# Filter taps from split operands, and the embedding's product moved from the state space scan to its set-up

## The chip, the cores and the metric

The kernel runs on one core of a Trainium2 chip. The metric is the device time of one launch in microseconds (us). The kernel before took 3740.24 us, the median of three runs (3736.25 to 3745.21). All other times here come from one further execution that the hardware profiler recorded.

## The reference, cut to what matters

One encoder layer over 2048 tokens of width 1024. After a norm, one input projection feeds four token mixers; their outputs go through an output projection, a feed-forward block and a gated per-layer embedding. Three pieces touch the change.

```python
def hyena_filter_spectrum(l, w1, b1, w2, b2, w3, log_decay):
    ...
    hid = jnp.sin(feats @ w1.astype(f32) + b1.astype(f32))
    hid = jnp.sin(hid @ w2.astype(f32) + b2.astype(f32))
    h = hid @ w3.astype(f32)                       # the filter taps: [2048, 64] @ [64, 1024]
    h = h * jnp.exp(-jnp.exp(log_decay.astype(f32))[None, :] * t[:, None])
    ...

# s5_mixer: the state space layer (set-up of the discretised matrices, then the scan)
# reference:
        gate = jax.nn.sigmoid(rmsnorm(h, g_ple[i]) @ w_ple_gate[i])
        h = h + gate * (p[i] @ w_ple[i])           # the embedding's product: [2048, 256] @ [256, 1024]
```

`p @ w_ple` depends on inputs alone, so it can be computed at any time before the last stage.

## The kernel before, in words

The program runs in three stretches. First the input projection (class `InProj`), then attention (class `Attention`) for the differential and the latent heads together, then output projection, feed-forward block and gated embedding, which all go through seven-product (Strassen) block multiplications. Attention works in 64 blocks, one head and 128 query rows each: 20 score products, 32 transposes and 32 weighings (each weighing shows as two pieces in the trace). With head h the keys and values are loaded again, so a head changes after every 16 blocks.

A float32 operand is often split into two parts, `hi` (rounded to the format float32r) and `lo` (the rest). A product of two split operands is then three products of parts (`mm3`, L52 to L54), each one piece on TensorE. A product of two unsplit float32 operands is issued once and shows as two pieces in the trace.

Beside the projection and the attention runs a queue of six background jobs (class `Background`). Each is a Python generator that yields estimated costs. At each of its steps, the main job lets the first job in the queue advance by a credit (`RATES`: 5.0 and 8.0 during the projection, 1.2, 1.2, 1.0 and 2.0 during attention). The jobs are the Hyena filters, the latent attention's preparation, the state space set-up with the short convolution, the state space main part (the scan, its output products and its gate) with the embedding, the Hyena long convolution, and the splitting of the output weights. `together(main, make, ..., every)` joins a second job to a first: after every `every`-th yield of the first, the second yields once, and what is left of the second runs when the first is done.

The framework then schedules all instructions by priority in a simulated timeline and fixes the order on each engine. TensorE (PE), VectorE (DVE), ScalarE (ACT), GpSimd (POOL) and SyncE (SP, which issues most DMAs) each execute in that order, so an instruction that waits holds up all that stand behind it on its engine.

Names used below: `f_hid` is the filters' hidden layer and `f_w` its weights (taps: L1113). `s5m_rows` holds the state space inputs loaded from DRAM (L1510), `s5m_u` their rearranged copy (ACT, L1522), transposed on PE at L1528. `d_s_m<-d_s_g` (L1507) are 16 DRAM-to-DRAM copies that spread the set-up's result. Scan instructions are L1567 to L1585 on POOL. The embedding's product is L52 to L54 on `wp_hi`/`wp_lo` and `pT_hi`/`pT_lo`, with transposes of `p_rows` (L946), copies into the tile `emb` (ACT, L954) and stores to DRAM (`d_emb`, L955). `emb` has one buffer.

Of the kernel before, what the change touches and what calls it, by code (L numbers as in the profile page):

```python
# [19 lines left out]
SEQ = 2048  # L20
# [1041 lines left out]
def hyena_filters(ops, const, A, S, cp, wk, ps_pool):  # L1062

    tc, nc = ops.tc, ops.nc
    dft = Dft16(ops, wk, 128, [nc.vector if e else nc.gpsimd for e in ENG[0]])
    feats = wk.tile([33, SEQ], F32, name="feats", tag="hy_a")
    nc.sync.dma_start(feats, A["c_feats"])
    w1 = cp.tile([33, 64], F32, name="f_w1")  # L1070
    nc.sync.dma_start(w1, A["hy_f_w1"][0])
    w2 = cp.tile([64, 64], F32, name="f_w2")
    nc.sync.dma_start(w2, A["hy_f_w2"][0])
    w3 = cp.tile([64, 1024], F32, name="f_w3")
    nc.sync.dma_start(w3, A["hy_f_w3"][0])
    bb = cp.tile([64, 2], F32, name="f_b")
    nc.sync.dma_start(bb[:, 0:1], A["hy_f_b1"][0].rearrange("(p o) -> p o", o=1))
    nc.sync.dma_start(bb[:, 1:2], A["hy_f_b2"][0].rearrange("(p o) -> p o", o=1))
    times = cp.tile([128, 16], F32, name="f_times")
    nc.sync.dma_start(times, A["c_times"])  # L1080
    ones = cp.tile([128, 128], F32, name="f_ones")
    nc.vector.memset(ones, 1.0)
    hid = cp.tile([64, SEQ], F32, name="f_hid")
    for layer, (w, src) in enumerate(((w1, feats), (w2, hid))):
        z = wk.tile([64, SEQ], F32, name="f_z", tag="hy_b")
        for c in range(4):
            ps = ps_pool.tile([128, 512], F32, name="ps_hy", tag="ps_hy")[:64]
            nc.tensor.matmul(ps, lhsT=w, rhs=src[:, ts(c, 512)], start=True, stop=True)
            nc.vector.tensor_scalar(z[:, ts(c, 512)], ps, bb[:, layer : layer + 1], None, ALU.add)
        for c in range(2):  # L1090
            k = wk.tile([64, 1024], F32, name="f_k", tag="f_mat", bufs=2)
            reduce_angle(nc, z[:, ts(c, 1024)], k)
        nc.scalar.activation(hid, z, AF.Sin)
        yield 10.0
    w3v = w3.rearrange("p (o d c) -> p o d c", o=2, d=2)

    def taps(od, hh):

        eld = wk.tile([128, 2, 128], F32, name="f_eld", bufs=1)
        for d in range(2):  # L1100
            nc.sync.dma_start(eld[:, d], A["hy_log_decay"][0:1, ds(512 * od + 256 * d + 128 * hh, 128)]
                              .to_broadcast([128, 128]))
        nc.scalar.activation(eld, eld, AF.Exp)
        h = wk.tile([128, 16, 2, 128], F32, name="f_h", tag="hy_a")
        part = wk.tile([128, 256], F32, name="f_part", bufs=1)
        nc.gpsimd.memset(part, 0.0)
        done.append((h, part))
        for t2 in range(8):
            ps = ps_pool.tile([128, 512], F32, name="ps_hy", tag="ps_hy")
            e = wk.tile([128, 512], F32, name="f_e", bufs=2)  # L1110
            for tt in range(2):
                t = 2 * t2 + tt
                nc.tensor.matmul(ps[:, ts(tt, 256)], lhsT=hid[:, ts(t, 128)], rhs=w3v[:, od, :, ts(hh, 128)],  # L1113
                                 start=tt == 0, stop=True, skip_group_check=True)
                nc.scalar.activation(e[:, ts(tt, 256)], eld.rearrange("p d c -> p (d c)"), AF.Exp,
                                     scale=times[:, t : t + 1])
            part_h = h[:, ts(t2, 2)].rearrange("p t d c -> p (t d c)")
            nc.vector.tensor_mul(part_h, ps, e)
            if t2 == 0:
                nc.vector.memset(h[0:1, 0, 1], 0.0)  # L1120
            nc.scalar.activation(e, part_h, AF.Abs)
            for tt in range(2):
                nc.gpsimd.tensor_add(part, part, e[:, ts(tt, 256)])
            yield 1.2

    done, groups = [], [(od, hh) for od in range(2) for hh in range(2)]
    yield from taps(*groups[0])
    for n, (od, hh) in enumerate(groups):
        h, part = done.pop()
        ps = ps_pool.tile([128, 512], F32, name="ps_hy", tag="ps_hy")[:, 0:128]  # L1130
        for d in range(2):
            nc.tensor.matmul(ps, lhsT=ones, rhs=part[:, ts(d, 128)], start=d == 0, stop=d == 1)
        skip = wk.tile([1, 128], F32, name="f_skip", bufs=1)
        nc.sync.dma_start(skip, A["hy_skip"][0, od : od + 1, ts(hh, 128)])
        norm = wk.tile([128, 128], F32, name="f_norm", bufs=1)
        nc.vector.tensor_copy(norm, ps)
        inv = wk.tile([128, 128], F32, name="f_inv", bufs=1)
        nc.vector.reciprocal(inv, norm)
        nc.vector.tensor_mul(norm[0:1], norm[0:1], skip)
        nc.vector.tensor_add(h[0:1, 0, 0], h[0:1, 0, 0], norm[0:1])  # L1140
        yield 6.0
        z = wk.tile([128, 2, 16, 128], F32, name="f_spec", tag="hy_b")
        for b in range(4):
            for a in range(2):
                f = wk.tile([128, 2, 4, 128], F32, name="f_mat", tag="f_mat", bufs=2)
                nc.sync.dma_start(f, A["c_dft_f"][:, b + 4 * a :: 8])
                ps = ps_pool.tile([128, 512], F32, name="ps_hy", tag="ps_hy").rearrange(
                    "p (t r c) -> p t r c", t=2, r=2)
                for i in range(2):
                    t = b + 4 * a + 8 * i  # L1150
                    for r in range(2):
                        mm = nc.tensor.matmul
                        mm(ps[:, i, r], lhsT=f[:, i, r], rhs=h[:, t, 0], start=i + r == 0, stop=False,
                           skip_group_check=True)
                        mm(ps[:, i, r], lhsT=f[:, i, 2 + r], rhs=h[:, -t % 16, 1], start=False,
                           stop=True, skip_group_check=True)
                for i in range(2):
                    nc.vector.tensor_mul(z[:, :, b + 4 * a + 8 * i], ps[:, i],
                                         inv[:, None, :].to_broadcast([128, 2, 128]))
                yield 2.0  # L1160
            eng = dft.engines[b]
            s = wk.tile([128, 2, 4, 128], F32, name="f_s", bufs=1)
            yield from dft.four(eng, z[:, :, b::4], s, False)
            if b:
                dft.rotate(eng, z[:, :, b::4], s, b, False)
                yield 2.0

        ahead = taps(*groups[n + 1]) if n < 3 else iter(())
        for ka in range(4):
            s = wk.tile([128, 2, 4, 128], F32, name="f_s", bufs=1)  # L1170
            for cost in dft.four(dft.engines[ka], z[:, :, ts(ka, 4)], s, False):
                yield cost
                yield next(ahead, 0.0)
            for r in range(2):
                nc.sync.dma_start(S["hspec"][od, hh, r, ka::4].rearrange("b p c -> p b c"), z[:, r, ts(ka, 4)])
        yield from ahead
# [537 lines left out]
def tile_hybrid_encoder(ctx, tc, A, out):  # L1714
# [19 lines left out]
    def background(make, c_name, w_name, side=None):  # L1734
        def gen():
            with ExitStack() as c:
                small = pool(c, c_name, 1, side=side)
                work = pool(c, w_name, 1, side=side)
                yield from make(ops, const, A, S, small, work, bg_ps)
        return gen  # L1740

    ip, st = InProj(ops, A, S), Strassen(ops)
    with ExitStack() as ac:
# [6 lines left out]
        def together(main, make, c_name, w_name, every):  # L1750

            def gen():
                with ExitStack() as c:
                    side = make(ops, const, A, S, pool(c, c_name, 1, side="right"), pool(c, w_name, 1, side="right"), bg_ps)
                    for n, cost in enumerate(main()):
                        yield cost
                        if n % every == 0:
                            yield next(side, 0.0)
                    yield from side
            return gen  # L1760
# [1 line left out]
        bg = Background(tc)  # L1762
        bg.add(background(hyena_filters, "hf_c", "hf_w", "right"))
        bg.add(background(mla_prep, "mp_c", "mp_w", "right"))
        bg.add(together(background(s5_setup, "ss_c", "ss_w", "right"), hyena_conv, "hc_c", "hc_w", EMN[1]))
        bg.add(together(background(s5_main, "sm_c", "sm_w", "right"), embedding, "em_c", "em_w", EMN[0]))
        bg.add(background(hyena_main, "hm_c", "hm_w", "right"))
        bg.add(out_weights)
        ip.run(const, bg.advance, lambda: bg.until(4))
# [119 lines left out]
```

## Time and profile before

| | |
|---|---|
| median of three runs | 3740.24 us |
| profiled execution, own time | 3744.99 us |
| its span, first to last instruction | 3743.2 us |
| TensorE busy | 3423.1 us (91%) |
| VectorE busy | 2455.0 us (66%) |
| ScalarE busy | 1754.3 us (47%) |
| GpSimd busy | 1553.0 us (41%) |
| mean granted TensorE clock | 0.958 of full |

Busy time is the sum of recorded spans; matmuls overlap in the array, so what one costs the stream is the distance from its start to the next one's start and not its own duration. The input projection takes the time up to about 555 us, attention runs from there to about 1900 us, and the rest follows. In the order of time the background jobs are the filters (to 391 us), the latent preparation (to 584 us), set-up and short convolution (585 to 850 us), scan and embedding (850 to 1216 us), long convolution (1216 to 1620 us) and output weights (1620 to 1700 us).

### The profile page before, as it was taken

Reading aid. Unit: us, or ns where it says so; the run is one execution under the profiler, and the core shown is the slowest. Engines: PE = TensorE matmul, PEld = TensorE weight load, DVE = VectorE, ACT = ScalarE, POOL = GpSimd, SP = SyncE. Lnnn points to the kernel's source line nnn. Section 1 sums busy time; section 2 is a strip of 40 time slices with the busy share of each in tenths; the row PEclk is TensorE's granted clock in tenths of the full one; section 3 lists DMA queues with packets and bytes.
Section 4 is the critical chain, followed back from the end, with each engine's and each line's share of the span. In section 5 each row is a group of like instructions: output and inputs, shape, how many; then the busy total and the mean of one; then the engine's idle time right before and its main releaser. Section 6 shows DMA issues by size and latency. Waiting matters only on the chain. (4 is left out here: it accounts for less than half of the span.)

```text
span 3743.2 us, 56824 instructions
## 1 busy us (share of the span) xinstructions
PE 3423.1 (91%) x20582; PEld 2802.2 (75%) x20582; DVE 2455.0 (66%) x5109; ACT 1754.3 (47%) x2889; POOL 1553.0 (41%) x1423
## 2 busy tenths in 40 slices
PE   8999997887999899989999899999999987989787
PEld 6889875676778778767777678887888865867666
DVE  6667548974746455677667764447545578688877
ACT  5334316665667545577754443334333433333443
POOL 1324001681852022253355554445544544344554
PEclk9999997998999999999999899999999999999899
DMA  4544655327232795961054532223222254546554
GB/s 143 185 142 153 219 164 141 104 76 208 76 100 87 190 251 146 222 195 40 18 178 144 177 113 79 90 79 107 90 79 90 74 188 149 203 141 191 186 170 151
DMA packets 426698, 518.46 MB, mean 139 GB/s; under 512 B 117003, under 2 KB 319631, under 8 KB 422415
## 3 DMA queue, kind: packets, MB, share of 16 engines
q1 hardware_dynamic: 352368, 407.05, 36.8%
q10 hardware_dynamic: 74048, 107.76, 8.2%
q8 instruction: 163, 2.67, 0.3%
q14 instruction: 119, 0.97, 0.1%
HBM read 340.89 MB, written 178.01 MB: 139 GB/s over the span
## 5 line engine op out<-in xcount | busy, mean ns | idle before, releaser
L448 PE MATMUL ps_s<-k_sb,q_sb 96*128 96x512 f32 x1280 | 437.5, 444 | 53.8 <-DVE at_s L451 22.2
L823 PE MATMUL ps_st<-t_hi,s_hi 128*128 128x512 f32 x984 | 397.2, 404 | 51.8 <-DVE st_sum L850 21.2
L458 ACT ACTIVATE at_s<-at_s,least_s 128x2048 f32<-128x2048 f32 x192 | 384.2, 2003 | 88.3 <-DVE least_s L457 71.6
L453 DVE CUSTOM_DVE_ANT_0 at_s<-ps_s,strip 128x512 f32<-128x512 f32 x512 | 338.1, 685 | 111.2 <-PE ps_s L448 96.9
L823 PE MATMUL ps_st<-t_lo,s_hi 128*128 128x512 f32 x984 | 392.6, 399 | 10.3 <-DVE t_lo L41 10.2
L823 PE MATMUL ps_st<-t_hi,s_lo 128*128 128x512 f32 x984 | 391.7, 398 | 5.6 <-DVE s_lo L41 5.5
L40 ACT ACTIVATE s_hi<-s_raw 128x512 fp32r<-128x512 f32 (+1 forms) x336 | 206.8, 618 | 352.9 <-PE ps_st L823 290.4
L497 ACT ACTIVATE at<-ps_at 128x512 f32<-128x512 f32 x512 | 287.7, 595 | 164.0 <-PE ps_at L492 151.1
L472 POOL TENSOR_SCALAR at_s<-at_s,f 128x1024 f32<-128x1024 f32 (+1 forms) x48 | 89.9, 1872 | 659.9 <-DVE f L466 474.6
L41 DVE TENSOR_TENSOR s_lo<-s_raw,s_hi 128x512 fp32r<-128x512 f32 (+1 forms) x336 | 270.0, 806 | 137.7 <-ACT s_hi L40 137.5
L492 PE MATMUL ps_at<-ident,at_s 128*128 128x128 f32 x2048 | 318.4, 286 | 41.7 <-ACT at L497 31.8
L40 ACT ACTIVATE a_hi<-a_raw 128x512 fp32r<-128x512 f32 (+1 forms) x252 | 155.4, 618 | 403.2 <-PE ps_st L823 217.5
L492 PEld LDWEIGHTS ps_at<-ident,at_s 128*128 128x128 f32 x2048 | 250.9, 146 | 108.5 <-ACT at L497 43.4
L448 PEld LDWEIGHTS ps_s<-k_sb,q_sb 96*128 96x128 f32 x1280 | 230.6, 197 | 122.4 <-DVE at_s L451 37.4
L823 PE MATMUL ps_st<-b_hi,a_hi 128*128 128x512 f32 x656 | 263.8, 402 | 30.9 <-DVE st_row L912 12.3
L807 POOL TENSOR_TENSOR s_raw<-a_raw 128x512 f32<-128x512 f32 (+1 forms) x84 | 110.8, 1319 | 433.6 <-DMA a_raw<-d_g 148.7
L41 DVE TENSOR_TENSOR a_lo<-a_raw,a_hi 128x512 fp32r<-128x512 f32 (+1 forms) x252 | 235.3, 936 | 72.1 <-ACT a_hi L40 71.1
L502 PE MATMUL ps_o<-at,v_sb 128*64 128x128 f32 x4096 | 274.2, 287 | 4.4 <-ACT at L497 3.3
L823 PEld LDWEIGHTS ps_st<-t_hi,s_hi 128*128 128x128 f32 x984 | 190.4, 194 | 104.4 <-DVE st_sum L850 25.0
L502 PEld LDWEIGHTS ps_o<-at,v_sb 128*64 128x64 f32 x4096 | 239.5, 144 | 36.2 <-issue 23.3
L823 PE MATMUL ps_st<-b_lo,a_hi 128*128 128x512 f32 x656 | 261.3, 398 | 4.4 <-DVE b_lo L41 4.3
L823 PE MATMUL ps_st<-b_hi,a_lo 128*128 128x512 f32 x656 | 260.7, 397 | 0.0
(480 smaller groups left out, 8305.7 us busy)
## 6 DMA issues: line engine op xcount, KB each, us to landing
d_h<-st_row ACTq DMA_DIRECT2D x64, 512.0 KB, 3.2
st_row<-d_h SPq DMA_DIRECT2D x64, 512.0 KB, 4.3
a_raw<-in_w_gate_dram SPq DMA_DIRECT2D x44, 512.0 KB, 4.0
a_raw<-in_w_up_dram SPq DMA_DIRECT2D x44, 512.0 KB, 3.9
d_g<-st_row ACTq DMA_DIRECT2D x44, 512.0 KB, 2.9
f_mat<-in_c_dft_f_dram SPq DMA_DIRECT2D x32, 512.0 KB, 4.4
h_g<-in_c_hy_g_dram SPq DMA_DIRECT2D x32, 512.0 KB, 7.1
h_sp<-d_hspec SPq DMA_DIRECT2D x64, 256.0 KB, 6.9
```

The lines of the kernel that those rows point to most:

```text
L40: nc.scalar.activation(hi, src, AF.Copy)
L41: nc.vector.tensor_sub(lo, src, hi.bitcast(F32))
L448: nc.tensor.matmul(ps, lhsT=lhs, rhs=rhs[:, ts(c, 512)], start=n == 0, stop=n == len(products) - 1)
L453: nc.vector.tensor_tensor_reduce(dst, ps, at.strip[:, ds(1920 - 128 * self.t + 512 * c, 512)], self.slope, 3e38, ALU.add, ALU.min, least)
L458: nc.scalar.activation(s, s, AF.Exp, bias=least, scale=-1.0, accum_out=self.total[name])
L472: nc.gpsimd.tensor_scalar(s2[:, n:], s2[:, n:], f, 0.0, ALU.mult, ALU.add)
L492: self.turned[hd, g] = nc.tensor.transpose(ps[:, j], src[:, ts(4 * g + j, 128)], at.ident)
L497: nc.scalar.activation(tile, ps, AF.Copy)
L502: mm = lambda out, lhsT, rhs, first, last: nc.tensor.matmul(out, lhsT=lhsT, rhs=rhs, start=first, stop=last, skip_group_check=True)
L807: eng.tensor_add(s1, a21, a22)
L823: nc.tensor.matmul(bank, lhsT=l[x][:, c], rhs=r[y], start=first and c + k == 0, stop=c == kb - 1 and k == 2, skip_group_check=True)
```

## The change

Two edits that do not depend on each other.

First, the taps. The second hidden layer's weight is loaded twice side by side, so that this product gives the 64 hidden values twice, on partitions 0 to 63 and 64 to 127. After the sine a copy rounds all 128 rows to float32r; on the upper 64 rows the rounded value is then subtracted, which leaves the low part there. The last weight is no longer loaded whole: each of the four groups of taps loads its 256 columns twice, rounds them (`w_hi`, 128 rows) and forms the low part (`w_lo`, 64 rows). One product over 128 rows gives (hi + lo) times `w_hi`, one over 64 rows adds hi times `w_lo`.

Second, the queue. The embedding is joined to set-up and short convolution, no longer to the state space main part, which now runs alone.

```diff
-    w2 = cp.tile([64, 64], F32, name="f_w2")
-    nc.sync.dma_start(w2, A["hy_f_w2"][0])
-    w3 = cp.tile([64, 1024], F32, name="f_w3")
-    nc.sync.dma_start(w3, A["hy_f_w3"][0])
...
+    w2 = cp.tile([64, 128], F32, name="f_w2")
+    bb = cp.tile([128, 2], F32, name="f_b")
+    nc.sync.dma_start(bb[0:64, 0:1], A["hy_f_b1"][0].rearrange("(p o) -> p o", o=1))
+    for half in range(2):
+        nc.sync.dma_start(w2[:, ts(half, 64)], A["hy_f_w2"][0])
+        nc.sync.dma_start(bb[ts(half, 64), 1:2], A["hy_f_b2"][0].rearrange("(p o) -> p o", o=1))
...
-        nc.scalar.activation(hid, z, AF.Sin)
+        nc.scalar.activation(z, z, AF.Sin)
         yield 10.0
-    w3v = w3.rearrange("p (o d c) -> p o d c", o=2, d=2)
+    hid = cp.tile([128, SEQ], F32R, name="f_hid")
+    nc.scalar.activation(hid, z, AF.Copy)
+    low = hid[64:128]
+    nc.vector.tensor_tensor(low, z[64:128], low.bitcast(F32), ALU.subtract)
...
+        w = wk.tile([128, 256], F32, name="f_w3", bufs=1)
+        for half in range(2):
+            nc.sync.dma_start(w[ts(half, 64)].rearrange("k (d c) -> k d c", d=2),
+                              A["hy_f_w3"][0].rearrange("k (o d c) -> k o d c", o=2, d=2)[:, od, :, ts(hh, 128)])
+        w_hi, w_lo = wk.tile([128, 256], F32R, name="f_w3_hi", bufs=1), wk.tile([64, 256], F32R, name="f_w3_lo", bufs=1)
+        nc.scalar.activation(w_hi, w, AF.Copy)
+        nc.vector.tensor_tensor(w_lo, w[0:64], w_hi.bitcast(F32)[0:64], ALU.subtract)
...
-                nc.tensor.matmul(ps[:, ts(tt, 256)], lhsT=hid[:, ts(t, 128)], rhs=w3v[:, od, :, ts(hh, 128)],
-                                 start=tt == 0, stop=True, skip_group_check=True)
+                nc.tensor.matmul(ps[:, ts(tt, 256)], lhsT=hid[:, ts(t, 128)], rhs=w_hi,
+                                 start=tt == 0, stop=False, skip_group_check=True)
+                nc.tensor.matmul(ps[:, ts(tt, 256)], lhsT=hid[0:64, ts(t, 128)], rhs=w_lo,
+                                 start=False, stop=True, skip_group_check=True)
...
-        bg.add(together(background(s5_setup, "ss_c", "ss_w", "right"), hyena_conv, "hc_c", "hc_w", EMN[1]))
-        bg.add(together(background(s5_main, "sm_c", "sm_w", "right"), embedding, "em_c", "em_w", EMN[0]))
+        short = together(background(s5_setup, "ss_c", "ss_w", "right"), hyena_conv, "hc_c", "hc_w", EMN[1])
+        bg.add(together(short, embedding, "em_c", "em_w", EMN[0]))
+        bg.add(background(s5_main, "sm_c", "sm_w", "right"))
```

How this moves the instructions shows in the fixed order. On PE, in the first half of the projection, where the first taps stand (`ps_ip` are the projection's own products, `ps_tr` the transposes of its input), before:

```order
L54 MATMUL ps_ip<-w_hi,aT_lo 128x304
L1113 MATMUL ps_hy<-f_w_368,f_hid 128x256 x4
L98 MATMUL ps_tr<-ident,x_in 128x128 x8
L1113 MATMUL ps_hy<-f_w_368,f_hid 128x256 x4
L52 MATMUL ps_ip<-w_hi,aT_hi 128x304
```

and in the changed kernel:

```order
L52 MATMUL ps_ip<-w_hi,aT_hi 128x304
L1124 MATMUL ps_hy<-f_w_hi,f_hid 128x256 x2
L1126 MATMUL ps_hy<-f_w_lo,f_hid 128x256
L1124 MATMUL ps_hy<-f_w_hi,f_hid 128x256
L1126 MATMUL ps_hy<-f_w_lo,f_hid 128x256 x2
L1124 MATMUL ps_hy<-f_w_hi,f_hid 128x256
L1126 MATMUL ps_hy<-f_w_lo,f_hid 128x256
L98 MATMUL ps_tr<-ident,x_in 128x128 x4
```

The order counts a float32 product once (the trace shows two pieces of it), so 64 products of taps become 128 and 128 pieces stay 128.

On SP, where the state space main part begins, before (`k_sb` and `v_sb` are the next head's keys and values, `s5m_win` and `s5m_m` the scan's matrices, `d_s_g<-s_strip` the set-up's last stores):

```order
L1496 DMA d_s_g<-s_strip 16x496
L1516 DMA s5m_bglu<-in_s_b_glu_dram 128x256
L369 DMA k_sb<-d_kda 32x2048 x2
L1507 DMA d_s_m<-d_s_g 16x16x256 x16
L1510 DMA s5m_rows<-d_zs_58 128x4096
L1535 DMA s5m_win<-d_s_win 128x1024 x2
L369 DMA k_sb<-d_kda 32x2048
L371 DMA k_sb<-d_kmn 64x2048
L392 DMA v_sb<-d_vda 128x8x64
```

and in the changed kernel:

```order
L381 DMA q_sb<-d_qda 32x2x128 x3
L382 DMA q_sb<-d_qmn 64x2x128
L383 DMA q_sb<-d_qmr 32x2x128
L1525 DMA s5m_a_9132<-d_s_a_77 128x64
L1527 DMA s5m_wglu<-in_s_w_glu_dram 128x2x256
L1529 DMA s5m_bglu<-in_s_b_glu_dram 128x256
L955 DMA d_emb<-emb 128x512 x2
L1523 DMA s5m_rows<-d_zs_58 128x4096
L1548 DMA s5m_win<-d_s_win 128x1024 x2
L1609 DMA s5m_m<-d_s_m 128x2x512
```

The 16 copies and the head's keys and values now stand well ahead of `s5m_rows`, and the embedding's last two stores right before it.

On PE, at the first transposes of `s5m_u`, before:

```order
L492 MATMUL ps_at<-ident,at_s 128x128 x16
L492 MATMUL ps_at<-ident,at_s_9033 128x128 x16
L502 MATMUL ps_o<-at,v_sb 64x128 x32
L502 MATMUL ps_o<-diag,at_ones 64x128 x2
L1528 MATMUL ps_hy<-ident,s5m_u 128x128
L946 MATMUL ps_hy<-ident,p_rows 128x128 x4
L1528 MATMUL ps_hy<-ident,s5m_u 128x128 x11
L52 MATMUL ps_hy<-wp_hi_7892,pT_hi 128x512
```

and in the changed kernel:

```order
L448 MATMUL ps_s<-k_sb,q_sb 128x512 x5
L492 MATMUL ps_at<-ident,at_s_9844 128x128 x4
L502 MATMUL ps_o<-at,v_sb 64x128 x32
L502 MATMUL ps_o<-diag,at_ones 64x128 x2
L448 MATMUL ps_s<-k_sb,q_sb 128x512 x5
L1541 MATMUL ps_hy<-ident,s5m_u 128x128 x8
L448 MATMUL ps_s<-k_sb,q_sb 128x512 x8
L492 MATMUL ps_at<-ident,at_s 128x128 x8
```

The transposes stand in the midst of a head's blocks now, with score products on both sides; 25 score products, 40 transposes and 68 weighings stand between the embedding's last product and the first of them. Of the embedding's 256 PE instructions, 132 stand before the set-up's last one and 124 behind it.

## Rows read from the trace of the kernel before

**Rows 1.** The page: busy time, share of the span and instructions of each engine

```profile
PE 3423.1 (91%) x20582; PEld 2802.2 (75%) x20582; DVE 2455.0 (66%) x5109; ACT 1754.3 (47%) x2889; POOL 1553.0 (41%) x1423
```

**Rows 2.** Busy time by stretch; columns: stretch, length, engines, clock, DMA share, GB/s

```profile
100.00:550.00 450.00, 447.20 (x2587) 386.71 (x2586) 272.93 (x641) 150.58 (x368) 101.95 (x120) 1.00 0.54 171
558.00:700.00 142.00, 107.75 (x701) 81.91 (x703) 122.72 (x378) 84.66 (x105) 33.45 (x31) 0.80 0.47 133
700.00:850.00 150.00, 134.46 (x1320) 107.09 (x1317) 115.05 (x308) 105.89 (x157) 129.17 (x78) 0.98 0.27 94
850.00:904.00 54.00, 30.70 (x254) 25.09 (x253) 17.31 (x65) 22.86 (x35) 4.42 (x4) 0.75 0.86 237
925.00:1050.00 125.00, 115.18 (x888) 94.25 (x883) 87.58 (x208) 74.82 (x112) 108.81 (x242) 0.96 0.27 86
1050.00:1216.00 166.00, 157.54 (x1137) 129.57 (x1135) 91.08 (x242) 114.54 (x170) 61.45 (x54) 0.97 0.29 91
1749.50:1807.90 58.40, 53.92 (x483) 44.00 (x482) 39.83 (x135) 41.89 (x60) 20.81 (x16) 0.97 0.07 19
```

**Rows 3.** Timeline of PE, the first taps; columns: start, length, engine, line, tiles

```profile
60.21 1.99 PE L1113 MATMUL ps_hy<-f_w,f_hid 64*128 64x256 f32 x8
62.13 1.09 PE L98 MATMUL ps_tr<-ident,x_in 128*128 128x128 f32 x8
```

**Rows 4.** Timeline of PE, products of parts over 256 columns

```profile
528.12 0.28 PE L52 MATMUL ps_hy<-wkv_hi,ckv_hi 128*128 128x256 f32 x1
528.24 0.28 PE L53 MATMUL ps_hy<-wkv_lo,ckv_hi 128*128 128x256 f32 x1
```

**Rows 5.** Groups by line, shapes apart: count, busy time, mean ns, idle before

```profile
L41 DVE TENSOR_TENSOR w_lo<-w_raw,w_hi 128x512 fp32r<-128x512 f32 x48 | 35.1, 744 | 13.8 <-ACT w_hi L40 13.7
...
L52 PE MATMUL ps_hy<-wp_hi,pT_hi 128*128 128x512 f32 x64 | 27.6, 438 | 0.0
...
L954 ACT ACTIVATE emb<-ps_hy 128x512 f32<-128x512 f32 x32 | 19.2, 601 | 26.1 <-PE ps_hy L54 17.4 <-DMA d_emb<-emb 8.4 <-ACT s5m_x L1544 0.2
...
L41 DVE TENSOR_TENSOR pT_lo<-ps_hy,pT_hi 128x512 fp32r<-128x512 f32 x16 | 10.9, 684 | 33.6 <-ACT pT_hi L40 33.5
```

**Rows 6.** Timeline of PE, where the state space main part begins

```profile
886.84 0.48 PE L1528 MATMUL ps_hy<-ident,s5m_u 128*128 128x128 f32 x1 [20.99 <-ACT s5m_u L1522]
...
892.74 0.63 PE L52 MATMUL ps_hy<-wp_hi,pT_hi 128*128 128x512 f32 x1
893.17 0.63 PE L53 MATMUL ps_hy<-wp_lo,pT_hi 128*128 128x512 f32 x1
...
896.72 0.39 PE L54 MATMUL ps_hy<-wp_hi,pT_lo 128*128 128x512 f32 x1
896.95 0.40 PE L52 MATMUL ps_hy<-wp_hi,pT_hi 128*128 128x512 f32 x1
```

**Rows 7.** Timeline of SP's queue at the same place

```profile
851.62 11.36 SPq L1507 DMA_DIRECT2D d_s_m<-d_s_g  x16
863.07 0.69 SPq L1510 DMA_DIRECT2D s5m_rows<-d_zs  x1
```

**Rows 8.** Timeline of ACT at the same place

```profile
883.84 3.90 ACT L1522 ACTIVATE s5m_u<-s5m_rows 128x1024 f32<-128x1024 f32 x4 [17.64 <-DMA d_mixT<-o_sb]
```

**Rows 9.** The stores `d_emb`: from issue to landing, and who waited

```profile
  ACT emb L954: 8.4, 5
...
DMA to landing us min/median/max: 2.0/3.5/9.3
```

**Rows 10.** Timeline of PE, later head changes (blocks 33 and 49)

```profile
1244.37 1.97 PE L1214 MATMUL ps_hy<-hm_a,hy_v 128*64 128x128 f32 x16 [10.83 <-ACT h_z L1228]
...
1634.80 0.77 PE L448 MATMUL ps_s<-k_sb,q_sb 96*128 96x512 f32 x1 [6.84 <-DMA k_sb<-d_kmr]
```

**Rows 11.** The exponentials (L458) by stretch: six ACT instructions to a block

```profile
700.00:850.00 150.00, 54.40 (x54) 0.98 0.27 94
925.00:1050.00 125.00, 33.16 (x32) 0.96 0.27 86
```

More of the change, by code (lines that the diff above doesn't have):

```diff
@@ L1071, in hyena_filters @@
     nc.sync.dma_start(w1, A["hy_f_w1"][0])
-    w2 = cp.tile([64, 64], F32, name="f_w2")
-    nc.sync.dma_start(w2, A["hy_f_w2"][0])
-    w3 = cp.tile([64, 1024], F32, name="f_w3")
-    nc.sync.dma_start(w3, A["hy_f_w3"][0])
-    bb = cp.tile([64, 2], F32, name="f_b")
-    nc.sync.dma_start(bb[:, 0:1], A["hy_f_b1"][0].rearrange("(p o) -> p o", o=1))
-    nc.sync.dma_start(bb[:, 1:2], A["hy_f_b2"][0].rearrange("(p o) -> p o", o=1))
+    w2 = cp.tile([64, 128], F32, name="f_w2")
[4 more added lines that the diff above has]
+        nc.sync.dma_start(bb[ts(half, 64), 1:2], A["hy_f_b2"][0].rearrange("(p o) -> p o", o=1))
     times = cp.tile([128, 16], F32, name="f_times")
@@ L1082, in hyena_filters @@
     nc.vector.memset(ones, 1.0)
-    hid = cp.tile([64, SEQ], F32, name="f_hid")
-    for layer, (w, src) in enumerate(((w1, feats), (w2, hid))):
-        z = wk.tile([64, SEQ], F32, name="f_z", tag="hy_b")
+    z = feats
+    for layer, w in enumerate((w1, w2)):
+        n, src = 64 * (layer + 1), z
+        z = wk.tile([n, SEQ], F32, name="f_z", tag="hy_a" if layer else "hy_b")
         for c in range(4):
-            ps = ps_pool.tile([128, 512], F32, name="ps_hy", tag="ps_hy")[:64]
+            ps = ps_pool.tile([128, 512], F32, name="ps_hy", tag="ps_hy")[:n]
             nc.tensor.matmul(ps, lhsT=w, rhs=src[:, ts(c, 512)], start=True, stop=True)
-            nc.vector.tensor_scalar(z[:, ts(c, 512)], ps, bb[:, layer : layer + 1], None, ALU.add)
+            nc.vector.tensor_scalar(z[:, ts(c, 512)], ps, bb[0:n, layer : layer + 1], None, ALU.add)
         for c in range(2):
-            k = wk.tile([64, 1024], F32, name="f_k", tag="f_mat", bufs=2)
+            k = wk.tile([n, 1024], F32, name="f_k", tag="f_mat", bufs=2)
             reduce_angle(nc, z[:, ts(c, 1024)], k)
-        nc.scalar.activation(hid, z, AF.Sin)
+        nc.scalar.activation(z, z, AF.Sin)
         yield 10.0
-    w3v = w3.rearrange("p (o d c) -> p o d c", o=2, d=2)
+    hid = cp.tile([128, SEQ], F32R, name="f_hid")
+    nc.scalar.activation(hid, z, AF.Copy)
+    low = hid[64:128]
+    nc.vector.tensor_tensor(low, z[64:128], low.bitcast(F32), ALU.subtract)
     def taps(od, hh):
```

## The prediction, made before the changed kernel was run

> **What bounds the kernel now.** I read the busy shares first: PE has 91% of the span, the next engine 66% [rows 1]. The same by stretch shows where PE has time to spare [rows 2]. From 100 to 550 us, in the input projection, PE is busy for 447.2 of 450.0 us at full clock: whatever PE is spared there ends the projection earlier, and whatever DVE (272.9) or ACT (150.6) gets on top has room. In attention a block without a background job takes 58.4 / 4 = 14.6 us, 13.5 of them PE. Under the jobs it differs. From 558 to 700 us DVE is busy for 122.7 of 142 us, PE for 107.8 at 0.80 of its clock. From 700 to 850 us POOL (the set-up's multiplications) has 129.2 of 150, PE 134.5. From 925 to 1050 us POOL (the scan) has 108.8 of 125, PE 115.2. From 1050 to 1216 us PE leads again with 157.5 of 166. Then I looked for PE's longest waits in its timeline. The longest in the kernel stands where the state space main part begins: 20.99 us before the first transpose of `s5m_u` [rows 6]. Waits at two other head changes are 10.83 and 6.84 us [rows 10].
>
> **Taps.** Eight pieces run from 60.21 to 62.13 us [rows 3]: 0.24 us a piece, 0.48 a float32 product. 64 products make 30.7 us. The new ones are products of parts over 256 columns, which start 0.12 us apart [rows 4]: 128 x 0.12 = 15.4 us. PE is spared 15.3 us, all of it in the stretch where it is the bound. The bounds: should the second product, with its 64 rows, keep a float32 piece's 0.24 us, the sum is 64 x 0.12 + 64 x 0.24 = 23.0 and the gain 7.7; should turning from parts to float32 and back cost each of the 32 banks another 0.1 us that now goes (an estimate, from the 0.12 us of a piece), it is 18.5. I take 15.
>
> The rest of this edit is cover's business. New are a copy and a subtraction over 2048 columns (an operation of 512 columns takes DVE 0.74 us [rows 5], so about 3 us each) and four pairs over 256 columns (0.4 us each, 3 us together), under 10 us on engines with 177 and 299 us free in that stretch [rows 2]. They stand before the first taps, so those come some 6 us later; behind them PE has the projection's products. Without that cover it would be 6 us, once. The second layer's product has 128 instead of 64 columns of weights and the same 512 moving ones, so I count it at nothing. On SP one more small load stands at the start and eight of 256 columns with the groups, for one load of 1024 columns; PE has no wait in that stretch that a load could lengthen much.
>
> **The wait at the main part's start.** Before, SP issues 16 copies from 851.62 to 862.98 us, then `s5m_rows` at 863.07 [rows 7]; ACT starts on it at 883.84 [rows 8], 20.8 us after the issue, with the next head's keys and values in the same queue. PE stands for 20.99 us [rows 6], since all attention work in its order is behind that transpose. And the engine comes back slow: embedding products start 0.43 us apart at 893 us and 0.23 at 897 [rows 6], so some 9 us of work went at half speed, which cost 4 to 5 us. In the changed order the copies and the head's loads are long issued, and between the embedding's last product and the first transpose PE has 25 scores, 40 transposes and 68 weighings. That is 1.25 blocks, of the weighings 2: about 18 us at 14.6 us a block. `s5m_rows` now stands behind the embedding's last store. ACT's copy (0.6 us [rows 5]) and the landing (3.5 us in the median [rows 9]) come first, then 2 MB that took 20.8 us in a full queue and, by that same traffic of 237 GB/s [rows 2], need at least 9. ACT gets it after 13 to 25 us, and needs another microsecond. Bounds: a wait of 0 to 8 us. I take 3. Of 25 us, 22 go. The other end is that nothing goes: the wait stays at 21.
>
> [...]
>
> **The embedding's cover.** It is 192 products at 0.23 us and 64 transposes of about 0.12: 52 us of PE. Where it runs beside an engine that is behind, it is hidden; elsewhere it adds. Before, by the order, about a third lies under the scan, whose stretch is bound by POOL; the other two thirds lie where PE is full. After, by the order, 132 of 256 instructions stand under the set-up. Its 150 us hold nine blocks (54 exponential rows at six a block [rows 11]) and 15 us without PE, of which the embedding can fill perhaps 10; some 20 fall to the first stretch, where PE is idle a quarter of the time: 4 us hidden, against 1.3 us of DVE for `pT_lo` and 2 for the split weights [rows 5]. The other 124 run beside attention alone, exposed. What was hidden before: 5 to 10 us, in PE's 9.8 idle us of the scan's stretch. What the scan loses it gets back in part, because the order lays seven blocks over it and not the 5.3 of before [rows 11]. I take 8 us gained. [...]
>
> **Head changes.** The one after block 16 no longer hides in the long wait; at 6.84 us [rows 10] with embedding products beside it I count 3. The one after block 32 no longer coincides with the long convolution's start, whose 10.83 us stay; I count 4. Together +7, bounds 0 to 14.
>
> The sum: -15 - 22 - 8 + 7 = -38 us. Against the profiled execution's own 3744.99 us that is 3707; it lies 4.75 above the median of the runs, 3740.24, so on their scale 3702.
>
> **Rivals.** First, only the taps count: `s5m_rows` comes as late as before, PE waits about 20 us again, and the cover's gain pays for the head changes. 3740 - 15 = 3725. For it: the load sits behind a store that must land. Against: 18 us of attention work now stand in between.
>
> Second, the cover is worth more: the set-up's idle us are filled, the clock of the first stretch recovers from 0.80 to near 1, which gives back some 15 of its 142 us, and no new wait appears. 3740 - 15 - 25 - 25 = 3675. Against: only 20 embedding instructions stand early.
>
> Third, slower: ACT stands behind the single `emb` buffer. Each of 32 copies must wait until the last store has landed, and ACT's exponentials queue behind it, for which PE's transposes wait. Before, that was 8.4 us in 5 waits [rows 9], with the outputs spread over some 310 us (a store every 10 us). Now 124 instructions stand in four and a half blocks, one output every 5 us or so, against 3.5 us in the median and 9.3 at most [rows 9]. If every copy waited 2 us more than now and PE with it, 32 x 2 = 64 us come on top: 3702 + 64 = 3766. It decides the sign from 1.2 us a copy (38 / 32). Against: spacing is above the median landing.
>
> [...]
>
> **How the numbers follow.** Forecast 3702 us (3688 to 3716): 0.48. Only the taps: 0.22. More cover: 0.13. Fourth: 0.08. Slower: 0.09. A measurement of this kernel tells 0.2% (7.5 us) from no change, so faster ends at 3732.8: 0.48 + 0.22 + 0.13 and a little of the fourth make 0.84; same 0.08; slower 0.08. The range leaves out most of the slower case and the far half of the second rival: 3672 to 3736.
>
> **What would show it.** Taps in pairs 0.12 us apart and the projection over about 15 us earlier, near 540 us; a first transpose of `s5m_u` after a wait below 8 us; no stretch at 0.75 of the clock at that place; PE's idle share from 700 to 850 us halved; the scan's stretch near 120 us with seven blocks in it. I am wrong if PE has a new wait above 10 us, if ACT's `emb` copies wait for `d_emb` for more than 30 us in all, or if the projection ends where it did.

## The result and the profile after

The changed kernel takes 3764.06 us in the median of four runs (3761.77 to 3772.25), the kernel before 3741.28; the ratio is 1.0065, with a 95% interval of 1.0052 to 1.0077. The change costs some 23 us where 38 were forecast as gain. The profiled execution has a span of 3760.9 us against 3743.2.

The page's busy line of the changed kernel, to set beside [rows 1]; columns as there:

```profile
PE 3441.5 (92%) x20582; PEld 2808.7 (75%) x20582; DVE 2464.5 (66%) x5114; ACT 1757.5 (47%) x2894; POOL 1574.6 (42%) x1423
```

PE has as many matmul records as before (64 float32 products of two pieces became 128 of one) and is busy for 18 us more. To see where, I divided both spans at the same four events: the first score of attention, the first transpose of `s5m_u`, the first product of the long convolution, and the first score of the 56th block, behind which no job is left. The first fence is the kernel before, the second the changed one; columns as in [rows 2], the first line of each being the projection.

```profile
0.00:558.50 558.50, 538.78 (x3117) 462.99 (x3117) 341.45 (x778) 205.26 (x458) 115.30 (x145) 1.00 0.53 167
558.50:886.80 328.30, 256.55 (x2196) 201.05 (x2196) 246.94 (x725) 203.87 (x281) 167.05 (x112) 0.87 0.44 132
886.80:1229.30 342.50, 322.33 (x2357) 265.13 (x2357) 213.52 (x545) 226.63 (x333) 172.54 (x302) 0.96 0.34 100
1229.30:1749.50 520.20, 466.98 (x4158) 388.10 (x4158) 316.58 (x873) 299.40 (x435) 138.69 (x108) 0.94 0.71 181
```

```profile
0.00:562.10 562.10, 537.03 (x3096) 461.96 (x3096) 350.48 (x778) 206.82 (x461) 117.88 (x145) 1.00 0.52 164
562.10:959.50 397.40, 347.98 (x2737) 271.01 (x2737) 291.54 (x842) 255.09 (x365) 178.66 (x116) 0.92 0.48 150
959.50:1277.50 318.00, 275.73 (x2144) 226.78 (x2145) 203.07 (x528) 205.85 (x293) 188.95 (x308) 0.94 0.28 76
1277.50:1770.20 492.70, 442.13 (x3853) 363.68 (x3853) 285.79 (x777) 270.02 (x393) 124.40 (x98) 0.94 0.70 182
```

The lengths hold different numbers of blocks, so what compares is PE's idle time, length less PE's busy time. Up to the first transpose it falls from 71.8 to 49.4 us: the long wait of [rows 6] is gone. In the state space main part it doubles, 20.2 to 42.3. Behind that it goes from 53.2 to 50.6. Together 145.1 and 142.3: what the vanished wait gave, the next stage took back.

The wait itself did what was forecast. SP's queue, ACT and PE of the changed kernel at that place, against [rows 6 to 8]:

```profile
947.77 0.32 SPq L1523 DMA_DIRECT2D s5m_rows<-d_zs  x1
```

```profile
955.58 3.90 ACT L1535 ACTIVATE s5m_u<-s5m_rows 128x1024 f32<-128x1024 f32 x4 [1.41 <-DMA s5m_rows<-d_zs]
```

```profile
957.33 1.42 PE L448 MATMUL ps_s<-k_sb,q_sb 96*128 96x512 f32 x5
959.53 1.09 PE L1541 MATMUL ps_hy<-ident,s5m_u 128*128 128x128 f32 x8 [0.78 <-ACT s5m_u L1535]
```

From the load's issue to ACT's start it is 7.8 us where it was 20.8, and PE stands for 0.78 us where it stood for 20.99. The eight transposes take 1.09 us, as eight do at full clock in [rows 3]: no half clock here.

Not all of the 20.8 us was the load. In the DMA records of the kernel before its 128 rows of 16 KB have been moved by 874.7 us, 11.7 us after its issue. ACT started 9.1 us later, because two stores of attention's output stand ahead of `s5m_u` in its order:

```profile
880.69 2.95 ACTq L527 DMA_DIRECT2D d_mixT<-o_sb  x2
```

The two were issued at 880.69 and 883.12 us, right behind the landing of two loads of the next head's keys and values (880.62 and 883.10 us). In the changed order the next head's loads stand far ahead, and this part of the wait is gone too.

What did not come is the taps' gain. The timeline of PE in the changed kernel, inside a group of taps, against [rows 3]:

```profile
66.14 0.39 PE L1126 MATMUL ps_hy<-f_w_lo,f_hid 64*128 64x256 f32 x1
66.45 0.39 PE L1124 MATMUL ps_hy<-f_w_hi,f_hid 128*128 128x256 f32 x1
66.77 0.50 PE L1126 MATMUL ps_hy<-f_w_lo,f_hid 64*128 64x256 f32 x2
67.20 0.39 PE L1124 MATMUL ps_hy<-f_w_hi,f_hid 128*128 128x256 f32 x1
```

From a product of 64 rows to one of 128 and back it is 0.31 us from start to start, not the 0.12 of [rows 4]. Summed over all taps, from each start to the next one's, the 128 products take 36.6 us; the 128 float32 pieces before took 33.3.

### The profile page after: what moved, and what is told of

Same layout as the page of the kernel before. It is cut to its first block, busy times and chain, and to the rows that moved or that the text cites. A ratio compares the mean times of both kernels' runs of the same rounds, so it can differ in the third digit from the quotient of the medians.

```text
span 3760.9 us, 56814 instructions
## 1 busy us (share of the span) xinstructions
PE 3441.5 (92%) x20582; PEld 2808.7 (75%) x20582; DVE 2464.5 (66%) x5114; ACT 1757.5 (47%) x2894; POOL 1574.6 (42%) x1423
## 5 line engine op out<-in xcount | busy, mean ns | idle before, releaser
L458 ACT ACTIVATE at_s<-at_s,least_s 128x2048 f32<-128x2048 f32 x192 | 383.7, 2000 | 64.9 <-DVE least_s L457 58.2
L502 PE MATMUL ps_o<-at,v_sb 128*64 128x128 f32 x4096 | 283.1, 291 | 8.2 <-ACT at L497 6.5
```

Of the source, the lines that this page charges most:

```text
L458: nc.scalar.activation(s, s, AF.Exp, bias=least, scale=-1.0, accum_out=self.total[name])
L502: mm = lambda out, lhsT, rhs, first, last: nc.tensor.matmul(out, lhsT=lhsT, rhs=rhs, start=first, stop=last, skip_group_check=True)
```

## Experiments

The experiments fall into three groups (a, b and c), each with its own runs of the kernel before (medians 3740.9, 3747.3 and 3745.6 us), so ratios are what compares. Microseconds between kernels below are differences of ratios, times these medians.

**The two parts apart.** a1_taps has the filters' edit alone, a2_queue the two lines of the queue alone.

> Only the filters' part of the change; the queue of jobs is the old one. Theory R (a change of the number of rows between two weight loads costs: 128, 64, 128 rows by turns, 0.31 us a product in place of 0.12): the taps take 36.6 us of PE against 33.3, the head adds about 3, so 3741 + 3 to 9 = 3744 to 3750, and the queue's move carries the rest of the loss. Rival S (the two parts of the change lose together, by what the projection leaves over for attention): 3755 or more here already.

> Only the queue's part of the change; the filters are the old ones. If the loss lies in attention (the blocks took 1208 us in place of 1191): 3741 + 12 to 20 = 3753 to 3761. If the prediction's terms for the queue hold and the longer head and the projection's end spoil them: 3741 - 15 to 30 = 3711 to 3726.

Measured: a1 3744.79 us, ratio 1.0010 (0.9996 to 1.0023); a2 3751.94 us, ratio 1.0027 (1.0014 to 1.0040). Neither part gains. The queue alone costs 10 us, the taps nothing that can be told; together they cost 24, some 10 us more than the sum (0.0065 against 0.0037), as far as the ends of the intervals just allow; a4 below shows the same excess, larger. In a2 the stages read like the changed kernel's: PE idle 51.6, 42.4 and 52.5 us.

**Rows.** a3_taps128 and a4_both128 run the second product over all 128 rows: the small part of the weights times both parts of the hidden layer, which adds the product of the two small parts. a3 has the old queue, a4 the new one.

```
-        w_hi, w_lo = wk.tile([128, 256], ...), wk.tile([64, 256], ...)
-        nc.vector.tensor_tensor(w_lo, w[0:64], w_hi.bitcast(F32)[0:64], ALU.subtract)
+        w_hi, w_lo = (wk.tile([128, 256], ...) for part in ("hi", "lo"))
+        nc.vector.tensor_tensor(w_lo, w, w_hi.bitcast(F32), ALU.subtract)
-                nc.tensor.matmul(ps[:, ts(tt, 256)], lhsT=hid[0:64, ts(t, 128)], rhs=w_lo,
+                nc.tensor.matmul(ps[:, ts(tt, 256)], lhsT=hid[:, ts(t, 128)], rhs=w_lo,
```

> As the first run, but the second product of each tap runs over all 128 rows (the small part of the weights times both parts of the hidden layer), so no two neighbours differ in rows. Theory R: 128 products at 0.12 = 15 us, 18 below the old taps; less 3 for the head: 3741 - 12 to 18 = 3723 to 3729, and 17 to 22 below the first run. Rival (what holds a product back is the sum in the same PSUM region, or the hidden layer that both load): 0.31 stays and this run equals the first.

> The changed kernel with the second product over 128 rows. Theory R: 17 to 22 below the changed kernel's 3764, so 3742 to 3747; the queue's loss stays. If the queue's loss came from the projection's end (20 products of the latent preparation left over for attention, 8 us): this goes too, 3730 to 3738. If rows don't matter: 3764.

Measured: a3 3733.61 us, ratio 0.9973 (0.9961 to 0.9986); a4 3759.68 us, ratio 1.0050 (1.0036 to 1.0064). PE's timeline in a3 at the same place:

```profile
65.96 0.28 PE L1126 MATMUL ps_hy<-f_w_lo,f_hid 128*128 128x256 f32 x1
66.08 0.28 PE L1124 MATMUL ps_hy<-f_w_hi,f_hid 128*128 128x256 f32 x1
66.20 0.39 PE L1126 MATMUL ps_hy<-f_w_lo,f_hid 128*128 128x256 f32 x2
66.43 0.28 PE L1124 MATMUL ps_hy<-f_w_hi,f_hid 128*128 128x256 f32 x1
```

Twice the rows in every second product and 0.12 us in place of 0.31: nothing else was altered, so the change of rows is the cause, and the rival (the shared PSUM region, the shared hidden layer) is out. All taps take 15.7 us from start to start, 17.6 below the old ones, as forecast for the changed kernel. The weight loads show how. First a load in the changed kernel, between products of 64 rows, then one in a3, at the same place:

```profile
66.45 0.19 PEld L1124 LDWEIGHTS ps_hy<-f_w_hi,f_hid 128*128 128x128 f32 x1
```

```profile
65.97 0.19 PEld L1124 LDWEIGHTS ps_hy<-f_w_hi,f_hid 128*128 128x128 f32 x1
```

The first starts 0.31 us after the product before it (66.14) and together with its own (66.45); the second starts with the product before it (65.96), and its own follows 0.12 us later (66.08). Yet the kernel gains 0.27%, 10 us, and not 15, and stays above its range. The reason stands in the same stretch. The projection's busy time in a3, and PE's waits there (waiting engine and line, what it waited for, us in total, times, longest):

```profile
100.00:550.00 450.00, 435.59 (x2590) 386.78 (x2589) 283.58 (x642) 149.84 (x370) 106.96 (x120) 0.99 0.54 171
```

```profile
PE ps_hy L1145 <- POOL f_part L1136: 4.5, 2, 2.6
PE ps_tr L98 <- DVE x_in L93: 3.1, 2, 2.9
PE ps_hy L1166 <- DMA f_mat<-in_c_dft_f_dram: 2.7, 1, 2.7
```

PE is now idle for 14.4 of 450 us where it was for 2.8 [rows 2]: with the taps quicker, POOL's sum of them, DVE and the next load come late. Besides, in every kernel with the new filters 33 products of the latent preparation start after the first score, before it were 12; those 21 at 0.24 us are 5 us that go to attention. So the first score comes 6.2 us earlier (552.3 us), and 5 of these were only moved.

a4 missed its forecast. With the rows mended the changed kernel should have come 17 to 22 us lower; it is 6 us lower (1.0050 against 1.0065), less than the two intervals can tell apart. So most of the changed kernel's loss is not the taps'. The queue's move costs 10 us with the old filters (a2), 21 with the taps of 128 and 64 rows (the changed kernel against a1) and 29 with those of 128 rows (a4 against a3). From one profiled execution of each, from the first score of attention to that of the 56th block, with the time in which PE works while the clock's records grant it half of full speed (a share of 0.5):

| | length | PE idle | PE at work at half clock |
|---|---|---|---|
| kernel before; a2 | 1191.0; 1207.3 us | 145.1; 146.5 | 116.0; 135.8 |
| a1; changed kernel | 1188.4; 1208.1 | 137.8; 142.3 | 103.4; 130.0 |
| a3; a4 | 1189.9; 1213.9 | 137.9; 144.2 | 109.7; 144.1 |

Work at half clock takes about twice as long (0.43 against 0.23 us a product in [rows 6]), so half of the last column's rise is lost: 10, 13 and 17 us. With the idle time that makes 11 of 16, 18 of 20 and 23.5 of 24 us. With equal filters, then, the queue's move costs less by waits than by the clock. Why it costs more with the new filters stays open.

**The wait alone.** b1_lead leaves the embedding beside the scan and lets time pass between the main part's loads and its first transposes; b3_taps128_lead is the same with a3's taps.

```
     v.memset(half, -math.log(2.0))
+    for _ in range(20):
+        yield 1.0
```

> The kernel before, with 20 steps of cost 1.0 between the state space main part's loads and its first transposes, so that ten steps of the embedding and about two blocks of attention go to PE while the rows arrive; the embedding stays beside the scan. Theory W (the wait of 21 us can be had, what was lost is the embedding's cover of the scan): 3741 - 14 to 22 = 3719 to 3727, PE's idle time beside the scan stays at 20 us. Rival P (the wait taken away comes back in small waits and at the half clock wherever it is taken away): 3736 to 3746.

> The taps with both products over 128 rows, the old queue, and the 20 steps ahead of the first transposes. Theory W: the two gains add, 3734 - 14 to 22 = 3712 to 3720. Rival P: 3729 to 3739.

Measured: b1 3748.21 us, ratio 1.0010 (0.9996 to 1.0025); b3 3735.38 us, ratio 0.9975 (0.9960 to 0.9990), no better than a3: neither gains by the edit, as rival P had it (b1's kernel before lies 6 us above the 3741 that its ranges start from). The 21 us are gone, but PE's waits from 850 to 1050 us in b1 are now:

```profile
PE ps_hy L53 <- DVE wp_lo L41: 11.0, 1, 11.0
PE ps_hy L52 <- ACT emb L954: 8.7, 1, 8.7
PE ps_s L448 <- DMA k_sb<-d_kmr: 5.5, 1, 5.5
```

Two of them stand in the embedding, which now runs into its own buffers and weights. So the run says that a wait moved is not a wait saved; it doesn't settle what the wait was worth, since the edit brought waits of its own.

**Cover.** b2_half splits the embedding: 512 columns beside the set-up, 512 beside the main part. b5_twice makes it in both places in full.

```
-    for nh in range(2):
+    for nh in halves:
...
+        first, second = (lambda *a, nh=nh: embedding(*a, halves=[nh]) for nh in range(2))
+        short = together(background(s5_setup, ...), hyena_conv, "hc_c", "hc_w", EMN[1])
+        bg.add(together(short, first, "e0_c", "e0_w", EMN[0]))
+        bg.add(together(background(s5_main, ...), second, "em_c", "em_w", EMN[0]))
```

> The kernel before, with one half of the embedding (512 of 1024 columns) beside the set-up and the other beside the scan. If a bare scan is the loss: PE's idle time beside the scan between 20 and 42 us, about 30; with the wait of 21 us gone 3728 to 3740, with the wait still there 3745 to 3752. If it is the embedding beside the set-up that costs (ACT behind its one buffer): the set-up's blocks grow by half of what they grew in the queue's run, 3745 to 3750, with idle time beside the scan at 20.

> The kernel before, with the embedding made twice: beside the set-up into a second scratch array that nobody reads, and beside the scan as before. It adds 192 products at 0.235 and 64 transposes at 0.11, 53 us of PE work. Against the queue's run (3752), where the scan is bare, it tells what the scan hides: with 22 us hidden 3752 + 31 = 3783, with nothing hidden 3752 + 53 = 3805. Against the kernel before (3741), what the set-up hides: with the wait of 21 us gone 3741 + 32 = 3773, with nothing hidden 3794 or more.

Measured: b2 3722.63 us, ratio 0.9943 (0.9923 to 0.9964), the lowest of all kernels here and below all of my ranges; b5 3801.42 us, ratio 1.0154 (1.0132 to 1.0176). Busy time in b2: the three stages of attention, and last the scan (from the scan's first multiplication on POOL to its last).

```profile
556.60:874.20 317.60, 260.71 (x2116) 202.80 (x2117) 249.47 (x700) 201.59 (x283) 173.83 (x108) 0.91 0.47 147
874.20:1199.50 325.30, 301.25 (x2348) 250.32 (x2346) 214.69 (x553) 220.55 (x319) 177.17 (x304) 0.97 0.34 95
1199.50:1719.70 520.20, 476.14 (x4250) 395.09 (x4249) 319.92 (x890) 306.32 (x445) 137.26 (x110) 0.94 0.71 182
...
924.20:1044.80 120.60, 113.04 (x898) 93.89 (x897) 85.51 (x205) 78.66 (x114) 110.13 (x242) 0.99 0.30 94
```

Idle 56.9, 24.1 and 44.1 us, 125.0 in all against 145.1 before: the wait at the start is gone, and the second half keeps the scan covered. Some 9 us of the gain lie in the last stage, which the edit doesn't touch. And the execution that was profiled took 3711.58 us, 11 below b2's median, so the stage times flatter it.

b5 came out at the end of my expectations where nothing is hidden. An embedding of 53 us of PE costs 58 us beside the set-up when the main part has one too (1.0154 against 1), and 47 beside the main part when the set-up has one (1.0154 - 1.0027). If such costs add, which I didn't test, a kernel without any embedding would lie 47 us below the kernel before; b2 lies 21 below it, so its two halves cost 26 us. By that sum half of the work is hidden when it is spread, about a tenth when it is all beside the main part and nothing when it is all beside the set-up: the first pieces fill what there is to fill.

**Is it the scan's cover?** c3_half_late is b2 with the second half held back until the scan is over.

```
-                        if n % every == 0:
+                        if n >= start and n % every == 0:
...
-        bg.add(together(background(s5_main, ...), second, "em_c", "em_w", EMN[0]))
+        bg.add(together(background(s5_main, ...), second, "em_c", "em_w", 1, start=48))
```

> One half of the embedding beside the set-up, the other only from the scan's end, beside the layer's output: the scan is bare again, the wait at its start stays away. If the scan's cover is what counts: PE's idle time in the scan 18 to 20 us (7.5 with the half beside it), seven blocks in it, and 3727 to 3737. If only the wait at the start and the length of the embedding beside the set-up count: 3718 to 3726, as with the half beside the scan.

Measured: 3740.79 us, ratio 0.9989 (0.9978 to 0.9999), 17 us above b2. That is 5 us below its own kernel before, as the range for the scan's cover has it (4 to 14 below 3741). The edit also lets the second half advance after every yield, in place of every second one; behind the scan PE is idle for 10.1 us in c3 and 12.5 in b2, so the denser pace brought no more waits there. The scan in c3 and, in the second fence, in the changed kernel:

```profile
909.90:1036.80 126.90, 108.60 (x842) 87.42 (x841) 88.18 (x219) 73.00 (x102) 112.83 (x244) 0.92 0.20 58
```

```profile
989.40:1114.80 125.40, 105.53 (x856) 86.36 (x854) 90.53 (x225) 77.20 (x107) 115.21 (x244) 0.95 0.16 49
1114.80:1258.80 144.00, 128.85 (x973) 106.50 (x975) 85.43 (x225) 97.65 (x140) 67.09 (x56) 0.94 0.29 82
```

POOL is busy for 113 and 115 us of the scan and sets its length: 120 to 125 us covered (128.5 in b1), 125 to 131 bare, over all kernels here. Bare, PE is idle for 18.3 and 19.9 us of it, its granted clock at 0.92 and 0.95; with the outputs of 12 embedding pieces beside it (b2) 7.6 us, at 0.99. PE works at half clock for 16.3 us of c3's scan and 3.4 of b2's, which loses some 6 us; with 10.7 us more of idle time that is the 17 us between them. Between the changed kernel and the kernel before this second part is missing: 9.8 us at half clock in the one's scan, 10.2 in the other's. What PE waits for in the bare scan of the changed kernel, and in the covered scan of the kernel before:

```profile
PE ps_s L448 <- DVE four_s L453: 8.7, 3, 6.4
PE ps_at L492 <- ACT at L497: 3.9, 4, 2.5
PE ps_s L448 <- DVE at_s L451: 2.7, 8, 0.4
```

```profile
PE ps_s L448 <- DVE four_s L453: 5.9, 3, 3.4
PE ps_at L492 <- ACT at L497: 2.1, 3, 0.9
PE ps_hy L1603 <- DMA s5m_m<-d_s_m: 1.3, 1, 1.3
```

No new kind of wait: attention's own steps between PE, DVE and ACT, which the embedding's products had filled.

**The changed kernel mended, and the best of both.** c2_half_taps64 is the changed kernel with b2's queue, c1_half_taps128 a3 with b2's queue; their edits are those shown above.

> The changed kernel with one half of the embedding put back beside the scan; the taps stay as changed (128 and 64 rows by turns). If the bare scan is where the changed kernel lost: 3722 + 4 for the taps = 3722 to 3732, some 35 below the changed kernel's 3764. If it lost by the taps and the queue acting together: 3740 to 3752.

> Half of the embedding beside the set-up and half beside the scan, with the taps' two products over 128 rows. If the two gains add (21 to 25 us for the halves, 7 for the taps): 3741 - 28 to 32 = 3709 to 3713. If the projection's end and the blocks behind it spoil one of them, as with the changed kernel (8 us more than the sum of its parts): 3717 to 3725.

Measured: c2 3736.76 us, ratio 0.9980 (0.9971 to 0.9990), between its two ranges and 32 us below the changed kernel; c1 3728.29 us, ratio 0.9954 (0.9940 to 0.9968). Half an embedding back beside the scan turns the loss into a gain. But c1 doesn't reach the sum of a3 and b2 (0.9916), and isn't below b2. Its idle time in the three stages is near the changed kernel's up to the first transpose and 14 us above b2's in the last stage. From the first score to that of the 56th block c1 takes 1182.8 us and c2 1181.8, b2 1163.1: with the new filters PE is busy there for 9 to 12 us more, the 21 moved products among it, and idle for 7 to 11 us more. What gives the last stage its 44 to 59 us of idle time, and why it is at the upper end in c1 and c2, stays open.

**ACT behind one buffer.** c4_two_buffers gives the output rows two buffers in the changed kernel.

```
-                e = wk.tile([128, 512], F32, name="emb")
+                e = wk.tile([128, 512], F32, name="emb_out", bufs=2)
```

> The changed kernel with two buffers of their own for the embedding's output rows. If ACT standing behind the one buffer delays the exponentials (12.0 us of waits on the stores in 5 waits): 3764 - 6 to 12 = 3752 to 3758. If these waits lie beside other work: 3760 to 3768, as the changed kernel.

Measured: 3763.97 us, ratio 1.0053 (1.0037 to 1.0069), as the changed kernel within what the intervals tell. The copy in the changed kernel, to set beside [rows 5]:

```profile
L954 ACT ACTIVATE emb<-ps_hy 128x512 f32<-128x512 f32 x32 | 19.0, 594 | 27.0 <-DMA d_emb<-emb 12.0 <-PE ps_hy L54 7.7 <-issue 2.7
```

ACT stood 12.0 us behind stores in five waits, and with two buffers no wait on the stores is left among the copy's in the profile. The time stays within a few us: these waits lay in the main beside other work.

## Why the prediction was wrong, step by step

**Taps (-15): the sign was wrong.** This is the first failed step. "128 x 0.12 = 15.4 us" took the distance of products that all have 128 rows [rows 4] for products that have 128 and 64 by turns. Those are 0.31 us apart: +3.3 us in place of -15.3, outside my bounds of 7.7 to 18.5, since I bounded the streaming and forgot the weights. [Rows 3] held a warning that I averaged away: the eight pieces with 64 rows take 1.92 us up to the next start, but inside they are 0.216 us apart (the first gap is 0.32); the last one takes 0.31, and what follows it has 128 rows. a3, with the rows made equal, has the 15.7 us I had reckoned. In the changed kernel as a whole the step weighs less than it seems: there the mended rows bring 6 us (a4).

Between products of equal rows (a3) a weight load starts within 0.01 us of the start of the matmul before it (65.97 against 65.96 us) and runs beside it; between 128 and 64 rows (the changed kernel) it starts 0.31 us after it in the median, together with its own matmul. Of the 97 products of the taps there that follow one of other rows, none had its weights loaded ahead: each load starts 1 to 2 ns before its own matmul. Why the loads wait there, no run shows.

**Projection earlier by 15: no.** It was 3.6 us later, one of my own signs of being wrong: 3.3 us by the taps, 5.4 by more idle time, less 5 for the 21 products moved behind the first score. Of the idle time 2.7 us lie in the first 70 us, where the filters' longer head, which I had counted as covered, puts the first taps 5.5 us later. Even where the taps did give 17.6 us (a3), 12 went into waits behind POOL, DVE and a load. "Whatever PE is spared there ends the projection earlier" holds only as far as the next engine is ahead.

**The wait (-22): right in the number, and the path in part.** It is 0.78 us long; idle time up to the first transpose fell by 22.3 us. I had expected the load to take 13 to 25 us; it took 7.8. And I took all of the 20.8 us before for the load's, though [rows 8] names `d_mixT<-o_sb`: the last 9 us were ACT's, behind two stores. That this part went as well, with the next head's loads that the change moves ahead, was luck.

**The embedding's cover (-8): the sign was wrong.** This is the second failed step. I let the scan lose 5 to 10 us of cover, partly got back by two more blocks. Measured, idle time in the main part rose by 22.1 us, about 10 of it in the scan, 10 behind it and 2 ahead of it. c3, which holds half an embedding back until the scan is over, is 17 us above b2, and c2, which puts half back, 32 us below the changed kernel. The set-up did not fill, as the changed kernel's busy time shows against the same stretches in [rows 2]:

```profile
700.00:850.00 150.00, 135.35 (x1202) 105.05 (x1201) 107.02 (x264) 101.83 (x151) 122.89 (x69) 0.98 0.37 131
850.00:904.00 54.00, 45.88 (x369) 37.53 (x368) 28.86 (x86) 32.99 (x50) 13.22 (x12) 0.95 0.72 204
```

PE's idle time from 700 to 850 us is 14.7 us against 15.5, not halved, while from 850 to 904 us, where the long wait was, it is 8.1 against 23.3 and the clock 0.95 against 0.75. I counted what a stage could take, and 58 us for a whole embedding beside the set-up (b5) say that it takes hardly any on top. Seven blocks do fit into the scan, as the order had it; a block brings its own waits with it, where the embedding brought none to the scan of the kernel before (in b1 it did).

On the clock, the second price: half speed while PE works, summed over the three stages from the clock's records, is 130 us against 116. The vanished wait had been at half clock mostly while PE stood (19 of 27 us), which costs nothing more. Of the 14 us more, 14 lie behind the main part (54.3 against 40.5) and 2 in it, with 2 less ahead of it. Against a1, which has the same filters and the old queue, it is 27 us more: 16 in the main part and 23 behind it, less 12 ahead of it. The long wait of the kernel before was paid for in part twice: its clock's records stand at half from 868.1 to 895.4 us, 8.6 us past the wait's end, and PE works for 7.9 of those 8.6. A price of this kind I had weighed for the scan: 19 us on the 95 us of PE work in seven blocks, should the clock fall from 0.96 to the first stretch's 0.80 [rows 2]. That fall was my estimate, and no run shows it: the clock is 0.95 in the scan of the changed kernel and 0.91 to 0.95 in every bare scan here. I set the price aside for seven blocks that I took for enough work.

**Head changes (+7): no.** The wait of 10.83 us at the long convolution's start is gone, one of 5.0 us on the keys came beforehand; idle time behind the main part is 2.6 us less.

The sum as measured in the profile: first score 3.6 us later, the stretch from there to the 56th block 1208.1 in place of 1191.0 us, the rest 3.0 us shorter: +17.7. Of the 17.1 us, idle time gives -2.9, half clock about +7 (half of 14), the 21 products moved out of the projection +5 to 8; 5 to 8 us are not accounted for.

**The rivals.** The fourth (it doesn't do what it says: pieces with 64 rows dearer, bare scan slow), with a chance of 0.08, named both places and priced the scan at +20; its taps were still 11 us too cheap. No run shows the +20, which was to come by a clock of 0.80: the scan's clock is 0.95 in the changed kernel, and what the main part lost is 22.1 us of idle time, with 2 us more of work at half clock. The third, ACT behind one buffer, came out at 3766 us, next to the measured time, but c4 leaves its mechanism a few us at most: a number that agrees is no evidence.

## What to carry to other kernels

Put neighbours on PE that load the same number of rows: a product widened with useful rows to match cost 0.12 us here, an odd one between others 0.31 and its successor 0.31. Before work is moved from one stage to another, ask of each stage which engine sets its length: beside a scan that POOL sets, the first filler on PE was in part hidden here, and moving all of it away cost 10 to 29 us. Spread filler over all such stages rather than place it in one, and when a long wait goes, look for the small ones, and for the work at half clock, that replace it.

## What was not expected of the hardware

In the changed kernel no weight load of the taps with other rows than the product before it ran beside that product: 0.31 us from start to start in the median, for 128 to 64 rows as for 64 to 128, and 0.31 as well in the 28 places where a product of the projection follows. With 128 rows throughout (a3) it is 0.12 (256 columns, float32 parts). A shorter contraction between products of 128 rows was therefore no saving: there 64 rows cost more (0.31 us) than 128 (0.12).
